# Causal convolution stage: twelve tap products per tile on ScalarE, three more unsplit input tiles, the mean of six chunks on VectorE

## The chip, the cores and the metric

One NeuronCore of a Trainium2 chip runs the whole program. The metric is the device time of one execution in microseconds (us), as the median of several runs. Engines are named as in the profile: PE (TensorE, matmul; PEld is its weight load), DVE (VectorE), ACT (ScalarE), POOL (GpSimd) and SP (SyncE). ACT, DVE, PE, POOL and SP each carry out their own instructions in the order in which the program was laid out.

## The reference

256 tokens of 2048 features pass through two blocks. The first block is a conformer convolution with a gated feed-forward layer, on 272 rows (16 meta tokens are put in front); the second has attention, pooling and a product-key expert layer. The change lies in the convolution:

```python
def conformer_conv(h, w_in, b_in, w_dw, b_dw, ln_g, ln_b, w_out, b_out):
    u = h @ w_in + b_in
    a, g = jnp.split(u, 2, axis=-1)
    u = a * jax.nn.sigmoid(g)
    u = jnp.pad(u, ((0, 0), (CONV_WIDTH - 1, 0), (0, 0)))
    u = lax.conv_general_dilated(u, w_dw[:, None, :], ...) + b_dw
    u = layer_norm(u, ln_g, ln_b)
    u = jax.nn.silu(u)
    return u @ w_out + b_out
```

CONV_WIDTH is 31 and the convolution is depthwise: every channel has 31 taps of its own.

## The kernel before, in words

**Tiles.** Channels lie on partitions, tokens along the free dimension. The convolution stage (`conv_stage`, L338) runs 16 iterations, one per group i of 128 channels. Iteration i makes two matmul products of 128x272: tile 2i (the half a) and tile 2i+1 (the gate g). Each contracts 2048 features in 16 steps, and its weights come as two units of 128x1024 (512 KB): tile m uses the units 2m and 2m+1. The iterations' products are called a(i) and g(i) here.

**Split and unsplit.** A split tile has its weights written as high part plus low part: ACT rounds the unit (L69), DVE subtracts (L84), and PE makes three products per step (L410 to L412). An unsplit tile goes to PE as it came (L414), with no work on ACT or DVE. `W_IN_SPLIT` (L41) names the split tiles: 4, 6, ..., 30, so a(2) to a(15) are split, and a(0), a(1) and all g(i) are not.

**Weights in flight.** `Weights` (L46) keeps four buffers for units as loaded (NRAW) and seven for split ones. SP issues the loads in order (L61); a load waits until its buffer is free, which for a split unit is after L84 and for an unsplit one after PE's last product with it. `split_to` (L71) splits ahead of need.

**Evacuation.** `evac` (L420) takes the sigmoid on ACT (L425, sg) and multiplies on DVE (L427), which writes the padded tile `up`. It is called sg(i) and up(i) here.

**Taps.** In iterations 2 to 14, 8 of the 31 taps are products on ACT (L445, `products`): four into a buffer of `wk["a"]`, four into one of `wk["b"]`, and a DMA issued by POOL adds the second to the first (L447). The other 23 taps run on DVE (L465, L467, then L470 alternating between two accumulators, joined at L472). `finish(i)` (L449) folds the four partial sums on DVE with three additions (L452, L453, L454); in the loop it is called for the tile before. Iterations 0 and 1 have all 31 taps on DVE. The last, i = 15, has 16 taps as products with diagonal matrices on PE (`diagonal_taps`, L480, L485) and 15 on DVE; there `finish(14)`, `taps(15)` and `finish(15)` (L456 its last addition) are called in this order behind up(15) (L533 to L541).

**Moments and normalisation.** Sums and sums of squares of each tile go into two accumulators, by a DMA up to i = 11 and by PE for the others (L501, L503). After the last one the mean and the root are formed (L561 on, an order written out by hand). For chunks k from KM = 4 on, POOL issues six DMAs that add the negative mean to two chunks each (L568 to L570), and `scale` (L553) only multiplies; for chunks below KM DVE multiplies and adds. Silu and a split of the result follow (L559, L192, L193), and the next matmul, `w_out`, begins.

**Order.** Instructions are ordered per engine when the program is built: by priority, with splits and evacuations moved ahead (`high_priority`), among those that the builder expects to be ready. That order is fixed on the chip.

Of the kernel before, what the change touches and what calls it, by code (L numbers as in the profile page):

```python
# [6 lines left out]
F32 = mybir.dt.float32  # L7
# [3 lines left out]
ALU = mybir.AluOpType  # L11

P = 128
# [12 lines left out]


NUP, LAG = 4, 3
NACT = [0, 0] + [8] * 13 + [0]
NPE = {15: 16}  # L30
NA, NB2 = 3, 2
MDMA = 11
KM = 4
SPE, SPL, SPM, HI, SPL2 = 65, 66, 67, 70, (68, 68, 68, 69, 70, 70, 70, 70)

HG, HM, HS, HC2, HT, HV = 19, 38, 14, 6, 24, 8
# [1 line left out]
CH, BU = 4, 2.7  # L38
U1 = 120
ENDS = (0, 0, 512), (1, 0, 256), (1, 256, 256)  # L40
W_IN_SPLIT = range(4, 32, 2)  # L41
COLS = ["mix_pre", "b_a", "b_g", "b_dw", "ln_g", "ln_b", "b_out", "mix_post",
        "ffn_pre", "ffn_post", "n1", "n2", "misc"]

# [51 lines left out]
class Kern:  # L96
# [238 lines left out]
    def w_in_split(self, i):  # L335
        return i in W_IN_SPLIT

    def conv_stage(self):  # L338
        nc, A, W = self.nc, self.A, self.W
        with ExitStack() as ctx:  # L340
            pl = ctx.enter_context(self.tc.tile_pool(name="p1", bufs=1))
# [15 lines left out]
            sq = pl.tile([P, TM], F32, name="sq1")  # L357
            r1 = pl.tile([P, TM], F32, name="r1")
            acc2 = pl.tile([P, 2, TM], F32, name="acc2")
            for k in range(0, KD, 2):  # L360
                g = self.col("mix_pre")
                nc.scalar.activation(hg[:, k], h[:, k], AF.Copy, scale=g[:, k:k + 1])
                nc.vector.tensor_scalar(hg[:, k + 1], h[:, k + 1], g[:, k + 1:k + 2], None, op0=ALU.mult)
                if k == 0:
                    nc.scalar.activation(acc2, h[:, :2], AF.Square)
                else:
                    s2 = self.tmp.tile([P, 2, TM], F32, tag="sq", name=self.nm("sq"), bufs=2)
                    nc.scalar.activation(s2, h[:, k:k + 2], AF.Square)
                    nc.vector.tensor_tensor(out=acc2, in0=acc2, in1=s2, op=ALU.add)
# [16 lines left out]
            for b in range(NUP):  # L386
# [10 lines left out]
                                           in1=self.col("b_dw"), op0=ALU.mult, op1=ALU.add)  # L397
# [3 lines left out]
            def product(i):  # L401
                ps = self.acc()
                t = t0 + 2 * i
                for k in range(KD):
                    u, o = t + k // UB, (k % UB) * P
                    W.split_to(u)
                    if self.w_in_split(i):
                        wh, wl = W.H(u, o), W.L(u, o)
                        uh, ul = uhl[:, k, :TM], uhl[:, k, TM:]
                        nc.tensor.matmul(ps[:, :TM], wh, uh, start=k == 0, stop=False)  # L410
                        nc.tensor.matmul(ps[:, :TM], wh, ul, start=False, stop=False)
                        nc.tensor.matmul(ps[:, :TM], wl, uh, start=False, stop=k == KD - 1)  # L412
                    else:
                        nc.tensor.matmul(ps[:, :TM], W.raw[u][:, o:o + P], (hg if i < 4 else h)[:, k], start=k == 0,  # L414
                                         stop=k == KD - 1)
                        if k % UB == UB - 1:
                            W.load_to(u + NRAW)
                return ps

            def evac(i, pa, pg):  # L420
                sg = self.tmp.tile([P, 2 * TM], F32, tag="sq", name=self.nm("sg"), bufs=2)[:, :TM]
                if i < 2:
                    for ps in (pa, pg):
                        nc.vector.tensor_tensor(out=ps[:, :TM], in0=ps[:, :TM], in1=r1, op=ALU.mult)
                x = nc.scalar.activation(sg, pg[:, :TM], AF.Sigmoid, bias=self.col("b_g")[:, i:i + 1])  # L425
                up = ups[i % NUP]
                y = nc.vector.scalar_tensor_tensor(out=up[:, 30:], in0=pa[:, :TM], scalar=self.col("b_a")[:, i:i + 1],  # L427
                                                   in1=sg, op0=ALU.add, op1=ALU.mult)
                return x, y

            def tap(i, j):
                return ups[i % NUP][:, 16 + j:16 + j + T], dw[:, i, j:j + 1]

            def products(i):

                wk[i] = wk["a"][i % len(wk["a"])]
                for j0 in range(31 - NACT[i], 31, 4):
                    if j0 == 31 - NACT[i]:
                        pr = wk[i]
                    else:  # L440
                        pr = wk["b"][wk["n"] % len(wk["b"])]
                        wk["n"] += 1
                    for j in range(j0, j0 + 4):
                        x, w = tap(i, j)
                        nc.scalar.activation(pr[:, j - j0], x, AF.Copy, scale=w)  # L445
                    if j0 > 31 - NACT[i]:
                        nc.gpsimd.dma_start(out=wk[i], in_=pr, accum_op=ALU.add)  # L447

            def finish(i):  # L449
                if NACT[i]:  # L450
                    a, c = wk[i], conv[:, i]
                    nc.vector.tensor_tensor(out=a[:, :2], in0=a[:, :2], in1=a[:, 2:], op=ALU.add)  # L452
                    nc.vector.tensor_tensor(out=a[:, 0], in0=a[:, 0], in1=a[:, 1], op=ALU.add)  # L453
                    nc.vector.tensor_tensor(out=c, in0=c, in1=a[:, 0], op=ALU.add)  # L454
                if i in NPE:
                    return nc.vector.tensor_tensor(out=conv[:, i], in0=conv[:, i], in1=wk["p", i][:, :T],  # L456
                                                   op=ALU.add)

            def taps(i, j0=0, j1=31):

                c, s, n = conv[:, i], (conv[:, i], acc2[:, 0, :T]), 31 - NACT[i] - NPE.get(i, 0)
                for j in range(j0, min(n, j1)):
# [11 lines left out]
            def diagonals(i, j0, j1):  # L474
                for j in range(j0, j1):
                    d = wk["d"].pop()
                    nc.scalar.activation(d, self.ident, AF.Copy, scale=dw[:, i, j:j + 1])
                    wk[i, j] = d

            def diagonal_taps(i):  # L480

                js = range(31 - NACT[i] - NPE[i], 31 - NACT[i])
                wk["p", i] = self.acc()
# [9 lines left out]
            wk = {"n": 0}  # L493
# [12 lines left out]
            for i in range(16):  # L506
                pa = product(2 * i)
                if i < 15:
                    W.split_to(t0 + 4 * i + 5)
                pg = product(2 * i + 1)  # L510
                W.split_to(t0 + min(4 * i + 7, SPE))
                with self.tc.high_priority(offset=PRIO + (300 if i == 15 else 0)):
                    x, y = evac(i, pa, pg)
                if i == 15:
                    break
                if i == 1:
                    t = self.xp.tile([P, 8192], F32, tag="X", name="work")
                    chunk = lambda r: t[:, 1024 * r:1024 * r + 1024].rearrange("p (q t) -> p q t", q=4)
                    wk["a"], wk["b"] = [chunk(r) for r in range(NA)], [chunk(r) for r in range(NA, NA + NB2)]
                    wk["d"] = [t[:, o:o + P] for o in range(1024 * (NA + NB2), 7936, P)]  # L520
                    wk["m"] = [t[:, 7936:], acc2[:, 1, :T]]
                    for w, v in enumerate((0.0, D * 1e-5 / P)):
                        nc.vector.memset(wk["m"][w], v)
                if i == 14:
                    diagonals(15, 31 - NPE[15], 31)
                if NACT[i]:
                    products(i)
                taps(i)
                if i > 0:
                    finish(i - 1)  # L530
                if i >= LAG:
                    moments(i - LAG)
# [20 lines left out]
            def scale(k, w):  # L553
                c = conv[:, k:k + w]
                for op, t in ((ALU.mult, rb), (ALU.add, mb))[:1 if k >= KM else 2]:
                    nc.vector.tensor_tensor(out=c, in0=c, in1=t.unsqueeze(1).to_broadcast([P, w, T]), op=op)
# [4 lines left out]
            with self.tc.high_priority(offset=3 * PRIO), self.tc.manual_schedule(engines=ORDERED), \  # L561
# [3 lines left out]
                a, c = acc2[:, 0, :T], [conv[:, k] for k in range(4)]  # L565
                nc.vector.scalar_tensor_tensor(out=v, in0=mom[1], scalar=1.0 / D, in1=v, op0=ALU.mult, op1=ALU.subtract)
                nc.scalar.activation(mn, mom[0], AF.Copy, scale=-1.0 / D)
                for k in range(KM, KD, 2):  # L568
                    nc.gpsimd.dma_start(out=conv[:, k:k + 2], in_=mn.unsqueeze(1).to_broadcast([P, 2, T]),
# [936 lines left out]
```

## Time and profile before

| what | value |
|---|---|
| median of 3 runs | 3250.02 us (3248.82 to 3256.38) |
| profiled execution, its own time | 3248.8 us |
| its span on the core | 3246.9 us |
| mean granted TensorE clock | 0.995 of full speed |
| PE busy | 3213.8 us, 99% |
| DVE busy | 2313.5 us, 71% |
| ACT busy | 1740.9 us, 54% |
| POOL busy | 39.8 us, 1% |

The span is the time from the first to the last profiled instruction; the profiled execution's own time is 1.9 us longer. Busy times overlap between engines, and the idle time of one engine costs something only when it moves the end. Times below count from the start of the span.

### The profile page before, as it was taken

Reading aid. Unit: us, or ns where it says so; the run is one execution under the profiler, and the core shown is the slowest. Engines: PE = TensorE matmul, PEld = TensorE weight load, DVE = VectorE, ACT = ScalarE, POOL = GpSimd, SP = SyncE. Lnnn points to the kernel's source line nnn. Section 1 sums busy time; section 2 is a strip of 40 time slices with the busy share of each in tenths; the row PEclk is TensorE's granted clock in tenths of the full one; section 3 lists DMA queues with packets and bytes.
Section 4 is the critical chain, followed back from the end, with each engine's and each line's share of the span. In section 5 each row is a group of like instructions: output and inputs, shape, how many; then the busy total and the mean of one; then the engine's idle time right before and its main releaser. Section 6 shows DMA issues by size and latency. Waiting matters only on the chain.

```text
span 3246.9 us, 49725 instructions
## 1 busy us (share of the span) xinstructions
PE 3213.8 (99%) x18613; PEld 2826.3 (87%) x18613; DVE 2313.5 (71%) x4106; ACT 1740.9 (54%) x2951; POOL 39.8 (1%) x47
## 2 busy tenths in 40 slices
PE   9989999999999999999999999999999999999999
PEld 8978888888888889999988888888888888888888
DVE  8997765666666766665569997777776676666664
ACT  4446644444444644544355467777877444444442
POOL 0110000000000000000000000000000000000000
PEclk9999999999999999999999999999999999999999
DMA  6787465555655555555655667777777977777764
GB/s 205 203 204 219 161 189 188 187 187 190 188 186 186 175 182 176 176 175 182 202 188 178 202 213 227 226 229 234 231 227 239 316 261 247 241 246 232 232 197 155
DMA packets 244002, 672.14 MB, mean 207 GB/s; under 512 B 21920, under 2 KB 95152, under 8 KB 241456
## 3 DMA queue, kind: packets, MB, share of 16 engines
q1 hardware_dynamic: 211968, 616.09, 59.8%
q10 hardware_dynamic: 24832, 41.34, 3.4%
q0 software_dynamic: 6960, 11.54, 2.0%
q8 instruction: 146, 2.39, 0.3%
q14 instruction: 96, 0.79, 0.1%
HBM read 619.58 MB, written 37.77 MB: 202 GB/s over the span
## 4 chain that ended last, share of the span: by engine, by line
PE 92%; DVE 5%; DMA 2%; ACT 1%; issue 0%; SPq 0%; ACTq 0%; DVEq 0%
PE acc L168 33%; PE acc L169 17%; PE acc L1392 7%; PE acc L1391 7%; PE acc L1390 7%; PE acc L175 4%; PE acc L177 4%; PE acc L176 4%; PE acc L414 3%; DVE wh L84 1%; PE g L1327 1%; DVE conv L470 1%; DMA wr<-in_w_in_dram 1%; DVE acc L470 1%; PE acc L937 0%; PE acc L938 0%
## 5 line engine op out<-in xcount | busy, mean ns | idle before, releaser
L84 DVE TENSOR_TENSOR wh<-wr,wh 128x1024 fp32r<-128x1024 f32 x1062 | 1295.8, 1223 | 735.8 <-ACT wh L69 733.2
L69 ACT ACTIVATE wh<-wr 128x1024 fp32r<-128x1024 f32 x1062 | 1123.4, 1060 | 1269.0 <-PE acc L169 426.7
L168 PE MATMUL acc<-xn,wh 128*128 128x512 f32 x2301 | 807.9, 394 | 0.0
L169 PE MATMUL acc<-xn,wh 128*128 128x256 f32 x2301 | 643.5, 280 | 0.0
L168 PEld LDWEIGHTS acc<-xn,wh 128*128 128x128 f32 x2301 | 431.3, 187 | 94.2
L168 PE MATMUL acc<-n,wh 128*128 128x512 f32 x1405 | 494.6, 397 | 0.0
L169 PEld LDWEIGHTS acc<-xn,wh 128*128 128x128 f32 x2301 | 434.4, 189 | 0.0
L1391 PE MATMUL acc<-wh,hid 128*128 128x512 f32 (+1 forms) x1032 | 399.8, 387 | 0.0
L1392 PE MATMUL acc<-wh,hid 128*128 128x512 f32 (+1 forms) x1032 | 399.8, 387 | 0.0
L1390 PE MATMUL acc<-wh,hid 128*128 128x512 f32 (+1 forms) x1032 | 399.7, 387 | 0.0
L169 PE MATMUL acc<-n,wh 128*128 128x256 f32 x1405 | 394.5, 281 | 0.0
L168 PEld LDWEIGHTS acc<-n,wh 128*128 128x128 f32 x1405 | 264.9, 189 | 63.1
L169 PEld LDWEIGHTS acc<-n,wh 128*128 128x128 f32 x1405 | 266.5, 190 | 0.1
L175 PE MATMUL acc<-n,wh 128*128 128x256 f32 x899 | 258.6, 288 | 7.0 <-ACT n L657 7.0
L176 PE MATMUL acc<-n,wh 128*128 128x256 f32 x899 | 255.7, 285 | 0.0
L177 PE MATMUL acc<-n,wh 128*128 128x256 f32 x899 | 253.3, 285 | 0.0
L168 PE MATMUL acc<-mid,wh 128*128 128x512 f32 x693 | 244.4, 398 | 0.0
L1390 PEld LDWEIGHTS acc<-wh,hid 128*128 128x128 f32 x1032 | 193.8, 188 | 39.7
L1391 PEld LDWEIGHTS acc<-wh,hid 128*128 128x128 f32 x1032 | 193.8, 188 | 39.6
L1392 PEld LDWEIGHTS acc<-wh,hid 128*128 128x128 f32 x1032 | 193.8, 188 | 39.6
L169 PE MATMUL acc<-mid,wh 128*128 128x256 f32 x693 | 193.9, 280 | 0.0
L175 PEld LDWEIGHTS acc<-n,wh 128*128 128x128 f32 x899 | 174.0, 194 | 13.1 <-ACT n L657 7.8
(379 smaller groups left out, 4410.0 us busy)
## 6 DMA issues: line engine op xcount, KB each, us to landing
wr<-in_U_dram SPq DMA_DIRECT2D x256, 512.0 KB, 4.4
wr<-in_V_dram SPq DMA_DIRECT2D x256, 512.0 KB, 4.4
wr<-in_gate_dram SPq DMA_DIRECT2D x88, 512.0 KB, 3.6
wr<-in_up_dram SPq DMA_DIRECT2D x88, 512.0 KB, 3.6
wr<-in_down_dram SPq DMA_DIRECT2D x88, 512.0 KB, 3.6
wr<-in_w_out_dram SPq DMA_DIRECT2D x64, 512.0 KB, 4.6
wr<-in_gl_dram SPq DMA_DIRECT2D x64, 512.0 KB, 3.7
wr<-in_w_in_dram SPq DMA_DIRECT2D x63, 512.0 KB, 4.8
```

The lines of the kernel that those rows point to most:

```text
L69: self.K.nc.scalar.activation(self.hl[i][:, 0], self.raw[i], AF.Copy)
L84: nc.vector.tensor_tensor(out=h[:, 1], in0=r, in1=h[:, 0].bitcast(F32), op=ALU.subtract)
L168: nc.tensor.matmul(ps[:m, :2 * n], self.W.H(t, o, m), x[:, :2 * n], start=first, stop=False)
L169: self.mm = nc.tensor.matmul(ps[:m, :n], self.W.L(t, o, m), x[:, :n], start=False, stop=last)
L175: nc.tensor.matmul(ps[:, :n], self.W.H(t, o), x[:, :n], start=first, stop=False)
L176: nc.tensor.matmul(ps[:, :n], self.W.L(t, o), x[:, :n], start=False, stop=False)
L177: self.mm = self.end = nc.tensor.matmul(ps[:, :n] if one else ps[:, n:2 * n], self.W.H(t, o), x[:, n:2 * n], start=False, stop=last)
L414: nc.tensor.matmul(ps[:, :TM], W.raw[u][:, o:o + P], (hg if i < 4 else h)[:, k], start=k == 0, stop=k == KD - 1)
L470: nc.vector.scalar_tensor_tensor(out=t, in0=x, scalar=w, in1=t, op0=ALU.mult, op1=ALU.add)
L1390: nc.tensor.matmul(ps[:, :w], xh, wh, start=ee == 0, stop=False)
L1391: nc.tensor.matmul(ps[:, :w], xh, wl, start=False, stop=False)
L1392: nc.tensor.matmul(ps[:, :w], xl, wh, start=False, stop=ee == G - 1)
```

## The change

The three parts are these. Taps: iterations 2 to 14 have 12 taps as products on ACT; the third group of four stays in its own buffer, and `finish` adds it to the first on DVE in one 128x1024 addition. `wk["b"]` has three buffers for it, used in turn, and two of the diagonal matrices move to a new tile `dg`. Split: tiles 8, 16 and 24, which are a(4), a(8) and a(12), are no longer split. Mean: KM is 6, so chunks 4 and 5 get the mean on DVE and POOL issues five DMAs.

```diff
-NACT = [0, 0] + [8] * 13 + [0]
+NACT = [0, 0] + [12] * 13 + [0]
 NPE = {15: 16}
-NA, NB2 = 3, 2
+NA, NB2 = 3, 3
 MDMA = 11
-KM = 4
+KM = 6
...
-W_IN_SPLIT = range(4, 32, 2)
+W_IN_SPLIT = [i for i in range(4, 32, 2) if i % 8]
...
+            dg = pl.tile([P, 2, P], F32, name="dg")
...
                 wk[i] = wk["a"][i % len(wk["a"])]
-                for j0 in range(31 - NACT[i], 31, 4):
-                    if j0 == 31 - NACT[i]:
+                for n, j0 in enumerate((27, 23, 19)):
+                    if n == 0:
                         pr = wk[i]
                     else:
                         pr = wk["b"][wk["n"] % len(wk["b"])]
...
                     for j in range(j0, j0 + 4):
                         x, w = tap(i, j)
                         nc.scalar.activation(pr[:, j - j0], x, AF.Copy, scale=w)
-                    if j0 > 31 - NACT[i]:
+                    if n == 1:
                         nc.gpsimd.dma_start(out=wk[i], in_=pr, accum_op=ALU.add)
+                    elif n == 2:
+                        wk["c", i] = pr

             def finish(i):
                 if NACT[i]:
                     a, c = wk[i], conv[:, i]
+                    nc.vector.tensor_tensor(out=a, in0=a, in1=wk["c", i], op=ALU.add)
                     nc.vector.tensor_tensor(out=a[:, :2], in0=a[:, :2], in1=a[:, 2:], op=ALU.add)
...
-                    wk["d"] = [t[:, o:o + P] for o in range(1024 * (NA + NB2), 7936, P)]
+                    wk["d"] = [t[:, o:o + P] for o in range(1024 * (NA + NB2), 7936, P)] + [dg[:, j] for j in range(2)]
```

## Rows read from the trace of the kernel before

**Rows 1.** The page: span, and busy time of each engine.

```profile
span 3246.9 us, 49725 instructions
PE 3213.8 (99%) x18613; PEld 2826.3 (87%) x18613; DVE 2313.5 (71%) x4106; ACT 1740.9 (54%) x2951; POOL 39.8 (1%) x47
```

**Rows 2.** Busy time by stretch: PE, PEld, DVE, ACT, POOL; granted clock, DMA share, GB/s.

```profile
54.25:227.50 173.25, 173.25 (x1041) 156.59 (x1039) 169.49 (x387) 75.78 (x149) 31.48 (x36) 1.00 0.81 204
227.50:257.80 30.30, 18.05 (x94) 15.59 (x93) 29.84 (x71) 15.23 (x26) 4.62 (x7) 0.83 0.57 146
```

**Rows 3.** The chain that ended last: a(0) to g(1), g(2), g(3), g(4) (start, us, what).

```profile
21.12 19.82 PE acc L414 x86
...
46.92 7.33 PE acc L414 x32
60.25 7.33 PE acc L414 x32
73.58 7.33 PE acc L414 x32
```

**Rows 4.** PE in order of time: the last product g(15), diagonals, moments, w_out.

```profile
220.01 7.50 PE L414 MATMUL acc<-h,wr 128*128 128x272 f32 x32
239.03 9.14 PE L485 MATMUL acc<-up,work 128*128 128x256 f32 x32 [11.52 <-DVE up L427]
248.01 0.59 PE L491 MATMUL mom<-work,ones 128*128 128x256 f32 x2
252.35 0.70 PE L503 MATMUL mom<-conv,ones 128*128 128x256 f32 x2 [0.73 <-DVE conv L456]
257.78 0.36 PE L175 MATMUL acc<-silu,wh 128*128 128x256 f32 x1
```

**Rows 5.** ACT in order of time: sg(3), sg(4) and sg(14) with what stands before them.

```profile
70.94 1.06 ACT L69 ACTIVATE wh<-wr 128x1024 fp32r<-128x1024 f32 x1 [7.83 <-DMA wr<-in_w_in_dram]
71.91 0.47 ACT L425 ACTIVATE sg<-acc,cols 128x272 f32<-128x272 f32 x1
...
84.53 0.47 ACT L425 ACTIVATE sg<-acc,cols 128x272 f32<-128x272 f32 x1
...
223.70 1.06 ACT L69 ACTIVATE wh<-wr 128x1024 fp32r<-128x1024 f32 x1 [4.96 <-DMA wr<-in_w_out_dram]
224.66 0.47 ACT L425 ACTIVATE sg<-acc,cols 128x272 f32<-128x272 f32 x1
...
228.77 2.09 ACT L445 ACTIVATE work<-up,dw 128x256 f32<-128x256 f32 x5
```

**Rows 6.** DVE in order of time: a tap, a folding addition, a split, the next.

```profile
214.69 0.48 DVE L470 SCALAR_TENSOR_TENSOR conv<-up,dw,conv 128x256 f32<-128x256 f32 x1
215.08 0.68 DVE L452 TENSOR_TENSOR work<-work 128x512 f32<-128x512 f32 x1
215.68 1.22 DVE L84 TENSOR_TENSOR wh<-wr,wh 128x1024 fp32r<-128x1024 f32 x1
216.82 0.42 DVE L472 TENSOR_TENSOR conv<-conv,acc 128x256 f32<-128x256 f32 x1
```

**Rows 7.** DVE in order of time: up(14), up(15), finish(14), end of finish(15), scale(4).

```profile
225.93 0.50 DVE L427 SCALAR_TENSOR_TENSOR up<-acc,cols,sg 128x272 f32<-128x272 f32 x1
...
238.49 0.48 DVE L427 SCALAR_TENSOR_TENSOR up<-acc,cols,sg 128x272 f32<-128x272 f32 x1
...
243.22 0.67 DVE L452 TENSOR_TENSOR work<-work 128x512 f32<-128x512 f32 x1
...
251.88 0.42 DVE L456 TENSOR_TENSOR conv<-conv,acc 128x256 f32<-128x256 f32 x1
...
259.90 0.42 DVE L193 TENSOR_TENSOR silu<-conv,silu 128x256 fp32r<-128x256 f32 x1
260.46 0.69 DVE L556 TENSOR_TENSOR conv<-conv,r 128x512 f32<-128x512 f32 x1
```

**Rows 8.** POOL's DMA of tile 14, and landing times of these DMAs (median, 100 to 275 us).

```profile
231.16 0.86 POOL L447 DMA_DIRECT2D work<-work  x1 [10.89 <-ACT work L445]
work<-work POOLq DMA_DIRECT2D x10, 512.0 KB, 10.2
```

**Rows 9.** The chain that ended last, after the moments: the mean's DMA, scale, silu.

```profile
254.04 6.39 DMA conv<-r
260.46 0.70 DVE conv L556
...
263.10 0.50 PE acc L168
```

**Rows 10.** Granted clock in stretches (columns as in rows 2): the diagonals run here.

```profile
240.00:241.00 1.00, 1.00 (x4) 0.78 (x3) 1.00 (x3) 1.00 (x2) 0.00 (x0) 0.50 0.10 16
243.00:244.00 1.00, 1.00 (x6) 0.86 (x5) 1.00 (x3) 0.42 (x1) 0.00 (x0) 0.98 0.28 29
```

**Rows 11.** Weight loads, 180 to 215 us, and the longest in the chain that ended last.

```profile
DMA to landing us min/median/max: 3.9/5.2/9.9
...
176.06 10.70 DMA wr<-in_w_in_dram
```

## The prediction

> **What bounds the kernel now.** I read the page first. PE is busy 3213.8 of 3246.9 us [rows 1], so everything that is to be won is 33.1 us of PE idle time, plus whatever PE does slowly. The busy times by stretch say where it lies. From 54 to 227.5 us PE never stops; beside it DVE is busy 169.5 of 173.25 us and ACT only 75.8. From 227.5 to 257.8 PE works 18.05 of 30.3 us, at a mean clock of 0.83, while DVE is busy 29.84 [rows 2]. So there are two stages with two limits: PE while the input products run, DVE in the tail after them. What shortens DVE's list during the products wins nothing there; it counts only if the tail gets shorter.
>
> PE in order of time shows the tail: g(15) ends at 227.5, and the diagonal products wait 11.5 us for up(15) [rows 4]. Why up(15) is so late stands in ACT's order. The period is 73.58 - 60.25 = 13.33 us [rows 3], so g(14) ended at 214.2, but sg(14) ran at 224.66, 10.5 us late: in front of it stands the rounding of a weight unit needed two tiles on, which waited for its DMA [rows 5]. At the beginning, behind the unsplit a(0) and a(1), the delay was smaller: g(3) ended at 67.6 and sg(3) ran at 71.9, g(4) at 80.9 and sg(4) at 84.5 [rows 3, 5], 4.3 and 3.6 us. The delay is built up by splitting, and a late sg(14) makes up(14), its ACT products, their DMA and finish(14) late. That is the chain I follow.
>
> **Unsplit tiles.** An unsplit tile takes 7.33 us of PE, a split one 13.33 - 7.33 = 6.00 [rows 3]. Three tiles: 3 x 1.33 = 4.0 us more, and nothing hides it, for PE has no idle time there [rows 2]. The products end at 231.5 instead of 227.5.
>
> The Trainium skill (FP8 and Floating Point Precision, TensorE Precision Notes) says that a true fp32 product takes four passes through the array. Against the three products of a split step that would make 6.00 x 4/3 = 8.0 us a tile, 6.0 us in all, and a time 2.0 us later than mine; the trace does not agree, with 7.33, and the measured number decides.
>
> In return six splits go: on DVE 6 x 1.14 = 6.8 us (from the start of a split to that of the next instruction) [rows 6], on ACT 6 x 1.06 = 6.4 [rows 5]. Their worth is indirect: sg(2), sg(6) and sg(10) no longer have a rounding in front of them, and the delay starts anew from there.
>
> The number of loads that SP issues is unchanged, but the buffers of a(4), a(8) and a(12) now come free only as PE uses them, so the next split tile's units arrive later behind them on SP. The first can load 3.67 us into the tile (half of 7.33); it needs its landing, 1.06 for the rounding and 1.14 for the subtraction by 14.66 (two unsplit tiles). Landings take 3.9 to 9.9 us, 5.2 in the median, at worst 10.7 [rows 11]; 8.8 are allowed. Cost: 0 by the median, 1.9 us by the worst; the second unit, free at 7.33 and needed at 14.66 + 3.00, 2.6 by the worst. I take 0, since these two loads go out 3.67 us apart and not in a bunch.
>
> **Taps.** Per tile DVE loses four taps at 0.39 us and gets one 128x1024 addition. No such addition is in the trace; the nearest row is the split, a two-operand instruction of that size, 1.14. Twice the 128x512 addition would be 1.20 [rows 6]. I take 1.14: 1.56 - 1.14 = 0.42 us saved, 5.5 over 13 tiles. With the splits DVE is relieved of 12.3 us, enough to catch up with a PE that became 4 us slower. ACT gets 52 products at 2.09 / 5 = 0.42 us [rows 5], 21.7 us, into 97.5 us of idle time [rows 2]. DMAs are as many as before, and POOL's issue still follows the eighth product. A new wait: the second group of four writes a buffer that DVE's finish two tiles before must have read. If DVE is behind, ACT stands there, with the next roundings queued behind it: 0 to some 3 us a tile, inside ACT's idle time. I take 0.
>
> **The mean.** DVE gets one addition of 128x512, 0.60 us [rows 6], in front of silu(4). What it saves is the wait for the first DMA, which landed at 260.43 [rows 9]: DVE's instruction before ran from 259.90 to 260.32, scale(4) began at 260.46 [rows 7]. So 0.14 goes and 0.60 comes, and PE was waiting for just that chunk at 263.10 [rows 9]. Later DMAs move up by one place, which gives some of it back. Bounds: 0.3 gained to 0.6 lost; I take 0.3 lost.
>
> **The sum.** g(14) ends at 231.5 - 13.33 = 218.2. Tile 24 is the last unsplit one, two iterations before 14, as a(1) is before 3; so I take the delay of sg(3) and sg(4), 4.0 us, and not 10.5: sg(14) at 222.2. up(14) follows 1.27 later, as before [rows 5, 7], at 223.5. POOL issued tile 14's DMA 231.16 - 225.93 = 5.2 us after up(14), and these DMAs land in 10.2 [rows 7, 8]: 238.9. finish(14) comes before taps(15) in the program, so DVE waits there; before, it began at 243.22. From there to the last addition of finish(15) it was 251.88 - 243.22 = 8.66 us [rows 7]; with the new addition 9.8. That gives 248.7 instead of 251.88, 3.2 us earlier. PE must keep up: behind up(15) 9.14 us of diagonals and 3.6 of moments [rows 4] ask for up(15) by about 235.5; 12.56 us after up(14), as before [rows 7], is 236.1, less 0.42 saved. It just fits. With the mean: 3.2 - 0.3 = 2.9 us won. Behind this stage PE is the limit, so the gain stays to the end: 3248.8 - 2.9 = 3245.9 for the profiled execution. The median of the runs lies 1.2 above that execution: **3247 us**.
>
> A measurement of this kernel can tell about 0.3% from no change, 9.75 us. The forecast lies within it.
>
> **Rivals.**
>
> *A: the evacuation becomes prompt.* If no rounding stands in front of sg(14), up(14) comes 1 us behind its product, at 219.2, and the DMA lands at 234.6: 244.4, 7.5 us earlier. If taps(15) run while finish(14) waits, up(15) at 232.5 is the start, and the diagonals follow an idle time of 1.5 us instead of 11.5. Before, they ran at half clock, 1.2 GHz, until 243 and at full clock after it [rows 10]. At the spacing of the moments' products, 3.6 us for eight [rows 4], 16 diagonals take 7.2: the last moments can begin at 232.5 + 0.5 + 7.2 + 3.6 = 243.8 instead of 252.35, 8.5 earlier, the best that this rival gives. Time: **3242**. For it: DVE is relieved of 12.3 us. Against it: sg(3), soon after unsplit tiles, was already behind a rounding [rows 5].
>
> *B: the delay stays (slower).* One place: the rounding in front of sg(14), whose DMA lands late. At 10.5 us of delay up(14) comes at 230.0, the DMA lands at 245.4 and the end is at 255.2, 3.3 later: 3250 + 3.3 + 0.3 = **3253.6**. It turns into a loss from a delay of 7.2 us on. For it: 10.5 us were standing at sg(14), and ACT's order is fixed when the program is built. Against it: the delay needs splits one after another to grow, and only a(13) to a(15) follow tile 24.
>
> *C: PE starves behind the unsplit tiles.* With the worst landing, 10.7, PE waits 2.6 us after each of three tiles, 7.8: 3254.9 with the forecast's tail, **3261** with B's. It decides from a landing of 8.8 us on. Against it: the loads are spaced, and behind g(1), which ended at 40.9, g(2) began at 46.92 [rows 3], after the 6.0 us of a(2) and no wait.
>
> **How the numbers follow.** Forecast 0.50, A 0.25, B 0.15, C 0.10. The likeliest gives 3247. Its range reaches to A's best end, 8.5 us and the mean's 0.3 below 3250 with some 0.7 for the spread of the runs, on one side, and past B on the other; only C with B lies outside: 3240.5 to 3254. Over 0.3% faster needs A's best end and a favourable mean, 0.06; over 0.3% slower needs C with B, 0.06; the rest, 0.88, is within.
>
> **What would show it.** Right: PE's products end near 231.5, with no idle time before; DVE shows 13 additions of 128x1024 near 1.2 us and is idle at times before 227; sg(14) some 4 us behind g(14); an idle time of DVE before finish(14)'s first addition, ended by a DMA; the last addition of finish(15) near 248.7; no DMA wait at scale(4). A shows in an idle time of PE before the diagonals of under 2 us and a clock that stays up. B shows in a DMA wait of ACT before sg(14) with 8 us or more. C shows in idle PE at the starts of a(5), a(9), a(13). The forecast is wrong if the tail from the products' end to the w_out product, 30.3 us before [rows 2, 4], is not between 21 and 28.

## The result: slower by 1.2%, and the profile after

The changed kernel is called after, and the runs of the experiments are numbered 1 to 13.

| | before | after |
|---|---|---|
| median of the runs beside each other (4 each) | 3250.64 us | 3288.59 us |
| ratio, 95% interval | | 1.0121 [1.0100, 1.0142] |
| span of the profiled execution | 3246.9 us | 3282.4 us |

The forecast was 3247 us, the range 3240.5 to 3254, and "slower" had a chance of 0.06. It is outside.

The page of the kernel after, span and busy time of each engine, answers to [rows 1]:

```profile
span 3282.4 us, 49624 instructions
...
PE 3225.3 (98%) x18565; PEld 2829.1 (86%) x18565; DVE 2304.7 (70%) x4062; ACT 1755.2 (53%) x2997; POOL 38.7 (1%) x46
```

DVE has 8.8 us less work and PE 11.5 us more, but the span grew by 35.5 us: most of it is idle time. Busy time by stretch (PE, PEld, DVE, ACT, POOL; then granted clock, DMA share, GB/s) shows where, against [rows 2]:

```profile
54.25:227.50 173.25, 155.04 (x829) 136.02 (x829) 143.69 (x313) 77.96 (x169) 30.02 (x35) 0.95 0.70 179
227.50:257.80 30.30, 25.67 (x149) 22.45 (x147) 17.78 (x36) 8.73 (x17) 0.86 (x1) 1.00 0.51 137
```

PE, which had no idle time in the first stretch, now has 18.2 us of it, and DVE, which was meant to be relieved, is idle for 29.6 us instead of 3.8. Who waits, and for what, stands in the list of waits of DVE and of PE, 40 to 330 us (total, times, longest):

```profile
DVE work L456 <- DMA work<-work: 38.6, 7, 7.5
...
PE acc L490 <- DVE up L428: 14.1, 1, 14.1
PE acc L411 <- ACT wh L69: 11.2, 1, 11.2
PE acc L413 <- DVE wh L84: 8.0, 5, 3.6
PE mom L508 <- DVE conv L461: 3.5, 1, 3.5
```

L456 is the new 128x1024 addition, now the first instruction of `finish`. In seven tiles DVE stands there for the DMA that adds the second group of products to the first. The same list of the kernel before names no wait for that DMA. One period of after shows it, DVE in order of time (start, duration, instruction, idle time before it and what ended it): up(9), its last tap, finish(9), up(10).

```profile
167.76 0.49 DVE L428 SCALAR_TENSOR_TENSOR up<-acc,cols,sg 128x272 f32<-128x272 f32 x1
...
176.36 0.49 DVE L475 SCALAR_TENSOR_TENSOR conv<-up,dw,conv 128x256 f32<-128x256 f32 x1
182.98 1.23 DVE L456 TENSOR_TENSOR work<-work 128x1024 f32<-128x1024 f32 x1 [6.13 <-DMA work<-work]
...
185.63 0.43 DVE L459 TENSOR_TENSOR conv<-conv,work 128x256 f32<-128x256 f32 x1
185.98 0.50 DVE L428 SCALAR_TENSOR_TENSOR up<-acc,cols,sg 128x272 f32<-128x272 f32 x1
```

POOL's issue of tile 9's DMA in after, and for comparison that of tile 11 (the tenth of 13) in the kernel before:

```profile
172.84 0.86 POOL L449 DMA_DIRECT2D work<-work  x1 [4.05 <-ACT work L447]
```

```profile
190.13 1.05 POOL L447 DMA_DIRECT2D work<-work  x1 [10.23 <-ACT work L445]
```

In after DVE is through with its taps 4.0 us behind the issue (176.85 against 172.84) and has nothing in front of finish(9). In the kernel before, finish(11) is the row at 215.08 in [rows 6], 25 us behind its DMA's issue, so a landing of 10 us never made DVE wait. The DMA did not become slower (8.6 us in the median of ten in after, 10.2 before [rows 8]); DVE came earlier. The order of DVE's instructions in the two traces says the same: before, finish(i) stands behind up(i+2) and amid the last taps of tile i+1, because DVE had a backlog of taps. In after, from tile 6 on, it stands directly behind the taps of tile i and ahead of up(i+1).

The period of that tile is 185.98 - 167.76 = 18.2 us, against 13.33 of PE [rows 3]. How long DVE stands follows the landing, the time from the issue of the DMA to its completion. Landing times of the adding DMAs issued at 172.84, 190.11 and 206.01 us (each the only one of its stretch; last number):

```profile
work<-work POOLq DMA_DIRECT2D x1, 512.0 KB, 10.0
```

```profile
work<-work POOLq DMA_DIRECT2D x1, 512.0 KB, 7.7
```

```profile
work<-work POOLq DMA_DIRECT2D x1, 512.0 KB, 4.5
```

The waits of DVE behind them are 6.13 us, 3.89 us and none, which is the landing less the 4 to 5 us of work that DVE still had behind the issue. What becomes of such a wait shows around 200 us, in DVE, then ACT, then PE of after:

```profile
197.95 1.23 DVE L456 TENSOR_TENSOR work<-work 128x1024 f32<-128x1024 f32 x1 [3.89 <-DMA work<-work]
...
200.60 0.42 DVE L459 TENSOR_TENSOR conv<-conv,work 128x256 f32<-128x256 f32 x1
```

```profile
201.06 0.42 ACT L503 ACTIVATE s<-conv 128x256 f32<-128x256 f32 x1 [9.65 <-DVE conv L459]
201.38 0.47 ACT L426 ACTIVATE sg<-acc,cols 128x272 f32<-128x272 f32 x1
202.42 4.90 ACT L447 ACTIVATE work<-up,dw 128x256 f32<-128x256 f32 x12 [0.57 <-DVE up L428]
207.23 1.99 ACT L69 ACTIVATE wh<-wr 128x1024 fp32r<-128x1024 f32 x2
```

```profile
195.63 1.54 PE L415 MATMUL acc<-h,wr 128*128 128x272 f32 x6
208.32 0.60 PE L411 MATMUL acc<-uhl,wh 128*128 128x272 f32 x1 [11.15 <-ACT wh L69]
```

finish ends at 201.0; ACT's square (L503) waits for it, sg(11) stands behind the square, then come the twelve products and then the roundings for a(13). PE, through with g(12), stands for 11.15 us. Each engine is in order, so one late instruction on DVE holds up ACT's and PE's next work.

The sum goes by the end of the last moments and of the products, and by the first w_out product. PE of the kernel before, the row behind the one at 252.35 in [rows 4], then PE of after:

```profile
252.89 0.67 PE L503 MATMUL mom<-s,ones 128*128 128x256 f32 x2
```

```profile
246.64 7.50 PE L415 MATMUL acc<-h,wr 128*128 128x272 f32 x32
...
286.16 0.98 PE L508 MATMUL mom<-s,ones 128*128 128x256 f32 x2
...
292.69 0.36 PE L175 MATMUL acc<-silu,wh 128*128 128x256 f32 x1
```

The last moments end at 253.6 us before and at 287.1 in after: the products end at 254.1 instead of 227.5, 26.6 later, of which 4.0 are the longer unsplit tiles, 19.2 are waits of PE (11.2 and 8.0 in the list) and 3.4 are left. Part of the rest is the clock: after the wait of 11.15 us the granted clock was 0.50 from 208 to 211 us and 0.54 from 211 to 215, the 1.2 GHz level, and 1.00 again from 215 to 219. The tail from the products' end to the last moments grew from 26.1 to 33.0. There ACT of after shows a rounding ahead of sg(14), as in [rows 5], and DVE a wait at finish(14):

```profile
250.12 1.06 ACT L69 ACTIVATE wh<-wr 128x1024 fp32r<-128x1024 f32 x1 [4.33 <-DMA wr<-in_w_out_dram]
251.08 0.47 ACT L426 ACTIVATE sg<-acc,cols 128x272 f32<-128x272 f32 x1
```

```profile
274.21 1.23 DVE L456 TENSOR_TENSOR work<-work 128x1024 f32<-128x1024 f32 x1 [6.01 <-DMA work<-work]
```

### The profile page after: what moved, and what is told of

Read it like the earlier page. It is cut to its first block, busy times and chain, and to the rows that moved or that the text cites. A ratio compares the mean times of both kernels' runs of the same rounds, so it can differ in the third digit from the quotient of the medians.

```text
span 3282.4 us, 49624 instructions
## 1 busy us (share of the span) xinstructions
PE 3225.3 (98%) x18565; PEld 2829.1 (86%) x18565; DVE 2304.7 (70%) x4062; ACT 1755.2 (53%) x2997; POOL 38.7 (1%) x46
## 4 chain that ended last, share of the span: by engine, by line
PE 90%; DVE 4%; DMA 3%; issue 2%; ACT 1%; POOL 0%; SPq 0%; POOLq 0%; DVEq 0%; ACTq 0%
PE acc L168 33%; PE acc L169 17%; PE acc L1397 7%; PE acc L1395 7%; PE acc L1396 7%; PE acc L175 4%; PE acc L177 4%; PE acc L176 4%; PE acc L415 2%; DMA work<-work 1%; PE g L1332 1%; DVE wh L84 1%; PE acc L942 0%; PE acc L944 0%; PE acc L943 0%
```

## The experiments

In the expectations, theory 1 is the order on DVE and the wait for the adding DMA, theory 2 the units behind unsplit tiles that arrive too late for PE, theory 3 the twelve products on ACT that hold up the roundings, unless a run names others.

**One part alone (1 to 3).** The kernel before with one part of the change each.

```diff
-W_IN_SPLIT = range(4, 32, 2)
+W_IN_SPLIT = [i for i in range(4, 32, 2) if i % 8]
```

> The kernel before with only tiles 8, 16 and 24 unsplit. Theory 1 (DVE stands at the first addition of finish, because DVE caught up with PE and the adding DMA, some 10 us long, has not landed): here DVE is relieved of 6.8 us and PE is 4 us longer, so waits of DVE for that DMA begin late in the stage, 5 to 20 us in all; time 3252 to 3268. Theory 2 (unsplit tiles free their buffers late, the next split tile's units come late and PE starves): nearly the whole loss is here, 3278 to 3290, with PE idle behind a(4), a(8) and a(12) and no DVE wait for the adding DMA. Theory 3 (twelve products on ACT hold up the roundings behind them): only PE's longer products, about 3254.

For the second, the whole taps part (12 products, three buffers, the new addition) with the splits and KM as before.

> The kernel before with only the tap change (12 products, third group added by DVE). Theory 1: DVE is relieved of 5.5 us spread over 13 tiles, so its backlog mostly stays and the waits for the adding DMA are few, under 10 us in all; time 3248 to 3260. Theory 2: no unsplit tiles, so about 3248 to 3251. Theory 3: nearly the whole loss is here, 3275 to 3290, with PE waiting for splits whose rounding stood behind products on ACT.

```diff
-KM = 4
+KM = 6
```

> The kernel before with KM = 6 only. All theories: 3250 to 3252, the w_out product 0.1 to 0.5 us later behind the moments than before, no DMA wait at the scaling of chunks 4 and 5.

Splits alone: 3269.04 us, 1.0061 [1.0044, 1.0078]. Taps alone: 3264.84, 1.0044 [1.0027, 1.0060]. Mean alone: 3250.02 against 3248.08, 1.0003 [0.9993, 1.0012]. The differences are 21.0, 16.8 and 1.9 us, together 39.7, where the whole change cost 38.0: two parts that have nothing in common but that they relieve DVE lose about the same. Both lost more than theory 1 expected, the first by 1 us only: 3269 where it had at most 3268, and 3265 where it had at most 3260, with more waiting (25.1 and 22.1 us) than the 5 to 20 and the under 10 expected. In the list of waits of DVE, first of the splits alone, then of the taps alone, the same line appears; in the first, with no new addition at all:

```profile
DVE work L452 <- DMA work<-work: 25.1, 5, 6.2
```

```profile
DVE work L456 <- DMA work<-work: 22.1, 5, 5.8
```

In both, finish(i) moves ahead of up(i+1), from tile 7 on in the first and from about tile 10 on in the second. Theories 2 and 3 can't explain both, since the second has no more unsplit tiles than before and the first no more products on ACT.

**Calling finish later (4).** After, with `finish(i - 2)` called ahead of `products(i)` instead of `finish(i - 1)` behind `taps(i)`.

```diff
+                if i > 1:
+                    finish(i - 2)
                 if NACT[i]:
                     products(i)
                 taps(i)
-                if i > 0:
-                    finish(i - 1)
...
+                finish(13)
                 finish(14)
```

> The changed kernel with finish of a tile called two iterations later, ahead of the products, instead of one iteration later behind the taps: the same work, the same DMAs, but the adding DMA has some 13 us more before DVE needs it. Theory 1: DVE's waits for the adding DMA fall from 38.6 us to under 5, PE's waits during the input products from some 19 us to under 5, time 3244 to 3258. Theory 2: the buffers are as before, time 3280 to 3290. Theory 3: the products on ACT are as before, time 3280 to 3290.

3279.3 us, 1.0091 [1.0074, 1.0108]. The edit did not do what it was for: finish(i) still stood ahead of up(i+1) in tiles 6 to 12, and DVE still waited 27.8 us for the DMA. Where a call stands in the program doesn't fix the order, so this run decides nothing.

**An order edge (5).** After, with finish(i-1) bound behind the last tap of tile i by an order edge, which fixes the order of two instructions and adds no work (`taps` returns its last addition).

```diff
-                taps(i)
+                e = taps(i)
                 if i > 0:
-                    finish(i - 1)
+                    with self.tc.issue_after(e.ins):
+                        finish(i - 1)
```

> The changed kernel with one thing more: finish of tile i-1 may not be issued on DVE before the last tap of tile i (an order edge, no other work). In the run with the late call the builder had still put finish of tile i ahead of up(i+1) from tile 6 on, so that run did not test the order. Theory 1 (in that place DVE, and behind it the next evacuation, stand until the adding DMA of some 10 us has landed): the waits of DVE for the adding DMA are left at finish(14) alone, under 8 us instead of 38.6, PE waits under 3 us during the input products, time 3241 to 3253. Theory 2 (late buffers behind the unsplit tiles): PE still waits behind a(4), a(8) and a(12), time over 3265.

3254.95 against 3248.61 us, 1.0021 [1.0009, 1.0033]: with nothing changed but the order, a loss of 38.0 us became one of 6.3. Theory 1 had expected a little more, at most 3253 us and under 3 us of PE's waits, which were 3.9. The list of waits of DVE has one such wait left, at finish(14):

```profile
DVE work L456 <- DMA work<-work: 2.3, 1, 2.3
```

**The order of after in the kernel before (6).** `finish(i)` right behind `taps(i)`, and the next evacuation bound behind it.

```diff
...
-                if i > 0:
-                    finish(i - 1)
+                finish(i)
...
-                finish(14)
```

> The kernel before, same work, with finish of tile i forced ahead of up(i+1) on DVE, as the builder placed it in the changed kernel. Theory 1: each tile then makes a loop of up, eight products on ACT, the adding DMA of 10 us, finish and the next up, some 18 us instead of 13.3; less the 11 us that the evacuation was late anyway, 30 to 50 us are lost: 3278 to 3300, with 12 or 13 DVE waits for the adding DMA. Theory 2: nothing is unsplit here, so 3248 to 3256.

3258.51 us, 1.0032 [1.0022, 1.0042]: slower, but by 10 us, not by 30 to 50. The list of waits of DVE in this run:

```profile
DVE work L452 <- DMA work<-work: 2.8, 4, 0.9
```

The landings of these DMAs from 100 to 275 us (count, size, median), against the 10.2 of [rows 8]:

```profile
work<-work POOLq DMA_DIRECT2D x11, 512.0 KB, 5.6
```

The expectation missed because it took the landing of 10 us as given. Here finish(i) has 21 of the longer taps (L470) in front of it instead of 17, and the DMA lands in 5.6. So this order does not make the loss by itself: it needs a landing longer than the work that DVE has in front of finish, and the landing was another here. What the order would cost the kernel before at a landing of 10 us was not measured. The 10 us that were lost lie mostly in the tail: the products ended at 230.0, 2.5 us later than before, but up(15), bound behind finish(14), came at 250.2 instead of 238.5. What goes with the landing is in the last section.

**No DMA to wait for (7).** After, with all three groups in buffers of their own and both additions on DVE; eight more of the diagonal matrices move to `dg`.

```diff
-                        nc.gpsimd.dma_start(out=wk[i], in_=pr, accum_op=ALU.add)
+                        wk["e", i] = pr
...
+                    nc.vector.tensor_tensor(out=a, in0=a, in1=wk["e", i], op=ALU.add)
```

> The changed kernel with the second group of products added by DVE too, in one more 128x1024 addition per tile, and no adding DMA for the taps. DVE gets 13 x 1.14 = 15 us more. Theory 1: no DVE wait for a DMA of tap products, no PE waits over 1 us each, time 3243 to 3260 although DVE has more to do. Theory 2: over 3270.

3249.83 against 3248.61 us, 1.0005 [0.9996, 1.0015]. DVE got 13 more additions, and the loss of 38.0 us became one of 1.2, though the unsplit tiles, the twelve products on ACT and the mean are all still there. So these did not make the loss; in this form they cost no more than that. It is no faster than before either, for DVE is as full as it was (columns as above):

```profile
54.25:227.50 173.25, 171.78 (x962) 151.88 (x961) 170.86 (x358) 86.73 (x187) 20.89 (x24) 1.00 0.58 167
```

Whether the missing DMA or the fuller DVE took the loss away, this run can't tell, since in the kernel before a DVE that full met no wait. Run 5 tells it: there DVE's work is that of after and only the order differs.

**The edge with one part each (8, 9).** The order edge of run 5 on the splits alone and on the taps alone.

> The kernel before with tiles 8, 16 and 24 unsplit, as in the run that changed only this (3269), and the same order edge on finish. Theory 1: 3242 to 3254. Theory 2: 3265 to 3272, as without the edge.

> The kernel before with twelve products (third group added by DVE) and the order edge that keeps finish of tile i-1 behind the last tap of tile i; all splits as before. Without the edge this took 3265. Theory 1, now with the landing time in it (finish waits for the adding DMA, which takes 4.7 us with no weight load issued just before it and 10 us behind four of them): no DVE wait for that DMA but at finish(14), PE without waits during the input products, up(15) 3 to 6 us earlier than in the kernel before; time 3243 to 3251. If the twelve products on ACT cost something by themselves (theory 3), PE waits for splits remain and the time is over 3255.

Splits: 3253.54 us, 1.0014 [1.0005, 1.0024], instead of 3269 without the edge. Taps: 3243.98 against 3246.58, 0.9992 [0.9983, 1.0000], instead of 3264.8. In both most of the loss goes with the edge, and what is left of it belongs to the splits. In run 9 PE has no wait for a split at all, with the twelve products on ACT, so theory 3 falls here.

**The tail (10, 11).** Runs 9 and 5, with taps(15) ahead of finish(14), so that its DMA has time to land.

```diff
-                finish(14)
-                taps(15)
-                z = finish(15)
+                e = taps(15)
+                with self.tc.issue_after(e.ins):
+                    finish(14)
+                    z = finish(15)
```

> The same, and taps(15) ahead of finish(14), so that the last wait for the adding DMA is covered too. Theory 1: no DVE wait for the adding DMA at all, 1 to 3 us less than the run beside it, 3241 to 3250. If the time is bound elsewhere in the tail (diagonals on PE behind up(15)), the same time as the run beside it.

> The changed kernel with the order edge, and taps(15) ahead of finish(14). With the edge alone it took 3255, DVE stood 2.3 us at finish(14). Theory 1: 1 to 3 us less, 3251 to 3255; what is left above the kernel before is the longer unsplit tiles (4.0 us) and PE's waits behind a(8) and a(12) (6 us). If those waits came from the adding DMA after all, they shrink too.

3243.75 us, 0.9992 [0.9983, 1.0001], and 3255.24, 1.0027 [1.0018, 1.0036]: neither differs from its parent by more than the intervals, so the 1 to 3 us that theory 1 expected were not won. DVE's waits of 2.6 and 2.3 us at finish(14) are gone from both traces, and the time is not: in both DVE then waits 2.2 us for PE's moments instead.

**What is left of after (12, 13).** In run 5 PE still waited for splits, 3.9 us in all, in a(9) and a(13). There up(i) stood behind all taps of tile i-1 and a finish. Now up(i) is bound behind the first 8 taps of tile i-1 only, the other taps behind up(i), finish(i-2) behind them; run 12 on after, run 13 on the taps alone. The edit against after, with J1 = 8:

```diff
+                if i > 2:
+                    with self.tc.issue_after(y.ins):
+                        e = taps(i - 1, J1)
+                    with self.tc.issue_after(e.ins):
+                        finish(i - 2)
                 if NACT[i]:
                     products(i)
-                taps(i)
-                if i > 0:
-                    finish(i - 1)
+                e = taps(i, 0, J1 if i > 1 else 31)
...
-                finish(14)
-                taps(15)
+                e = taps(14, J1)
+                with self.tc.issue_after(e.ins):
+                    finish(13)
+                    finish(14)
+                    taps(15)
```

> The changed kernel with an order on VectorE in which up(i) stands behind only the first 8 taps of tile i-1, then the other taps of i-1, then finish(i-2). Theory 1 (what is left after the order edge is again the order: up(i) stands behind all taps of tile i-1 and a finish, so the sigmoid's tile comes late, and with it the roundings and splits behind it): up(7) and up(8) come within 4 us of the end of g(7) and g(8), the 2.21 us wait of TensorE for a split in a(9) goes, the products end at 231 to 233 (4.0 us of longer unsplit tiles remain), time 3246 to 3252. Theory 2 (the two units behind an unsplit tile land too late, whatever VectorE does): the waits at the starts of a(9) and a(13) stay, products end at 235 to 238, time 3253 to 3257. Theory 3 (twelve products on ScalarE hold the roundings): the waits stay too, but named as waits for L69, with the roundings right behind 12 products.

> The same order on VectorE in the version with the twelve products alone (tiles 8, 16, 24 split, mean as before). Theory 1: products end at 226 to 228 with no wait of TensorE, up(15) within 5 us of that; the tail then holds 11 more taps of tile 14, 4.3 us, so the last moments end at 248 to 252; time within 4 us of the kernel before, on either side. If up(15) is no earlier than in the version with the order edge alone (233.8), theory 1 is wrong about what holds it, and the time is 3248 to 3252.

Run 12: 3256.03 against 3248.32 us, 1.0021 [1.0011, 1.0032], no better than run 5 and above the 3246 to 3252 expected, though the part of the expectation about PE came true. Busy time by stretch, columns as above, then PE and ACT in order of time, in the tail:

```profile
54.25:227.50 173.25, 173.25 (x976) 153.81 (x975) 151.59 (x334) 89.26 (x188) 31.84 (x36) 1.00 0.76 201
```

```profile
228.61 2.68 PE L415 MATMUL acc<-h,wr 128*128 128x272 f32 x11
239.88 2.08 PE L490 MATMUL acc<-up,dg 128*128 128x256 f32 x4 [8.58 <-DVE up L428]
...
258.37 1.22 PE L508 MATMUL mom<-conv,ones 128*128 128x256 f32 x2 [4.85 <-DVE conv L461]
```

```profile
222.80 1.71 ACT L447 ACTIVATE work<-up,dw 128x256 f32<-128x256 f32 x4 [3.03 <-DVE work L456]
...
225.45 1.04 ACT L69 ACTIVATE wh<-wr 128x1024 fp32r<-128x1024 f32 x1
226.39 0.47 ACT L426 ACTIVATE sg<-acc,cols 128x272 f32<-128x272 f32 x1
```

PE is busy for the whole stretch, and its products end at 231.3, where the forecast had them, 231.5. So with this order neither the units behind the unsplit tiles nor the products on ACT held PE up. In run 5 the products did hold up roundings. ACT of run 5, then of run 11, the products of up(7) and the roundings for a(9):

```profile
130.14 4.89 ACT L447 ACTIVATE work<-up,dw 128x256 f32<-128x256 f32 x12 [0.57 <-DVE up L428]
134.94 1.99 ACT L69 ACTIVATE wh<-wr 128x1024 fp32r<-128x1024 f32 x2
```

```profile
126.54 4.90 ACT L447 ACTIVATE work<-up,dw 128x256 f32<-128x256 f32 x12 [0.57 <-DVE up L428]
131.34 1.04 ACT L69 ACTIVATE wh<-wr 128x1024 fp32r<-128x1024 f32 x1
132.92 1.06 ACT L69 ACTIVATE wh<-wr 128x1024 fp32r<-128x1024 f32 x1 [0.54 <-DMA wr<-in_w_in_dram]
```

In run 5 both roundings stand behind the products and neither waits for a load, so the units were there; what was late is up(7), and PE waited 2.2 us in a(9). Run 11 has the same order as run 5 on DVE, ACT and PE up to the end of the products, but there up(7) came 3.6 us earlier and PE didn't wait in a(9); its waits were 0.8 us in all, and the products ended at 232.0, not 237.2. So these waits also vary from one execution to the next by some 3 us, and that run 12's order, with up(7) at 122.8, removes them for good is likely, not shown by one trace. Waits in a(9) or a(13) show in runs 7 (1.5 us) and 8 (3.7) too, and none in runs 9, 10 and 13, which keep all splits. So theories 2 and 3 are not the loss, but unsplit tiles, with products in front of the roundings behind them, were worth some 1 to 4 us.

In run 12 the last moments end at 260.4 all the same, 6.8 us behind before: 3.8 from the products and 3.0 from a tail of 29.1 us. In the tail sg(14) ran at 226.4, 8.4 us behind g(14) (218.0); in front of it stand four products that waited 3.03 us for a buffer that finish two tiles back had yet to read, and a rounding. DVE had 11 taps of tile 14 still to do behind up(15), 4.3 us that the expectation for this run left out, though that for run 13 had them. How much of the tail each of the three costs was not told apart.

Run 13: 3243.07 against 3248.32 us, 0.9987 [0.9978, 0.9996]; up(15) at 230.0 and the last moments at 251.1, as expected. It is the best version found: about 4 us, or 0.13%, by the ratio, less than the 0.3% that the prediction names as what a measurement can tell from no change. Its profiled execution, at 3251.68 us, was the longest of its eleven, so these two moments are not those of a median one.

## Why the prediction was wrong

**What failed.** The step that failed is in "Taps" and "The sum": DVE relieved of 12.3 us (the page shows 8.8 us less busy time, the mean's addition in it) was booked as a gain ("enough to catch up"), and the wait of finish for its DMA in tiles 2 to 13 was put at nothing. DVE did catch up, and so it met a wait that its backlog had covered, 38.6 us in seven tiles, finish(14) among them. The prediction knew the DMA (issue 5.2 us behind up, landing 10.2 [rows 7, 8]) and knew that DVE would wait for it at finish(14). For the other twelve tiles it kept the old place of finish without saying so. With its own numbers the loss could have been found: behind up(i) DVE has some 9 us of work (17 taps at 0.39, two shorter ones and a split; 167.76 to 176.85 in after), the DMA lands 5.2 + 10.2 = 15.4 us behind up(i), so 6 us of waiting; then some 3 us of finish, and a period of 18, five more than PE's 13.33. That is the tile shown; where the landing was shorter, DVE waited less. The prediction's own sign of being wrong showed: from the products' end to the first w_out product it was 38.6 us (254.1 to 292.7), not 21 to 28. And one of its signs of being right, DVE idle at times before 227 us, came as the loss itself, 29.6 us. The question that was not asked: if DVE is no longer behind, what stands next in its list, and is that ready?

**Unsplit tiles, right.** 4.0 us more on PE. Without PE's waits the products ended at 231.3 (run 12), against 231.5 forecast. The Trainium skill (FP8 and Floating Point Precision, TensorE Precision Notes) has four passes for a true fp32 product. The prediction's estimate from that rule, 8.0 us a tile, would have ended the products at 233.5; run 12 speaks for the measured 7.33. That is no evidence against four passes as such: the estimate also takes each of the three products of a split step to cost as much as one pass, which no run tests.

**Late units, taken as 0: too low by 1 to 4 us.** PE waited in a(9) and a(13), rival C's place, in runs 5, 7, 8 and 11, the runs with unsplit tiles in which the large wait is gone, for 3.9, 1.5, 3.7 and 0.8 us; only in run 12 it did not. C's mechanism, a load that lands too late, doesn't show in a(9) of run 5: there the units had landed, and the roundings stood behind the products of a late up(7).

**The delay of sg(14), wrong.** Forecast 4.0 us. It was 11.7 in after (g(14) ended at 239.4, sg(14) ran at 251.08) and 7.8 in run 11, where g(14) ended at 218.7. ACT in order of time, run 11, then run 9, where g(14) ended at 212.9:

```profile
225.58 1.06 ACT L69 ACTIVATE wh<-wr 128x1024 fp32r<-128x1024 f32 x1 [4.45 <-DMA wr<-in_w_out_dram]
226.54 0.47 ACT L426 ACTIVATE sg<-acc,cols 128x272 f32<-128x272 f32 x1
```

```profile
219.10 1.06 ACT L69 ACTIVATE wh<-wr 128x1024 fp32r<-128x1024 f32 x1 [4.52 <-DMA wr<-in_w_out_dram]
220.06 0.47 ACT L426 ACTIVATE sg<-acc,cols 128x272 f32<-128x272 f32 x1
```

The reason given for 4.0 was that the delay grows by splitting and starts anew behind an unsplit tile. With the order edge it was 7.2 us in run 9, which keeps all splits, and 7.6 in run 5, which doesn't: the unsplit a(12) made it no shorter. The rounding in front of sg(14) is of a unit of w_out, in [rows 5] too, which PE needs only behind the moments, at 257.78 before [rows 4]; it waits for its load whatever is split. In run 13 that rounding waited for no DMA, and the delay was 3.7.

This is rival B's place, a rounding that waits for its DMA in front of sg(14). B had 0.15; it gave 3253.6, 3.6 above the kernel before, from a delay of 10.5, and became a loss from 7.2 on. Runs 5 and 11, in which the large loss is gone, came to 3255, 6.3 and 8.7 us above the kernel before beside them. So without the wait in DVE's list the time would have been nearer to B than to the forecast; how much of it is sg(14) and how much are PE's waits was not told apart.

**The new addition, right.** Taken as 1.14 us from the split; it runs 1.23, with 1.14 to the next instruction. The wait for a second group's buffer, taken as 0, was no matter in after, whose list of ACT's waits doesn't name it; it came up in run 12, 3.03 us in the row above.

**finish(14), right in kind.** DVE waits there for the DMA, 6.01 us in after, 2.3 in run 5. That removing it gains nothing (runs 10, 11) was not forecast.

**The mean, not contradicted.** Forecast 0.3 us lost; alone it measured 1.9, with an interval that holds zero and 0.3 alike. The wait for the first DMA of the mean is gone there, and no gain shows.

**The frame, half right.** "What shortens DVE's list during the products wins nothing there" held. That it can lose there was missing. The rivals for a slower outcome, B and C, looked at ACT, SP and PE, none at DVE, the engine that the change relieves.

## What to carry to other kernels

A backlog on an in-order engine hides the latency of whatever it will consume next. Before you lighten such an engine, list what it consumes from DMAs and from other engines, and work out how long after the issue it will get there without the backlog. Where the builder orders by expected readiness, bind the consumer of a slow transfer behind independent work with an order edge, and read the order off the built program, since moving the call may change nothing (run 4).

## What the runs showed of the hardware

**Landing behind weight loads.** The same DMA, 512 KB added to a buffer on the chip, landed in 4.5 to 12.5 us. Around the issue of the one of 10.0 us in after, at 172.84, SP issued four weight loads of 512 KB, three in the 5 us before it and one 0.2 us behind its start:

```profile
167.88 5.52 SPq L61 DMA_DIRECT2D wr<-in_w_in_dram  x4
```

Ahead of the one of 4.5 us there was none in that time. In the kernel before, too, four stood ahead of the one at 190.13, and it landed in 10.0; so that is the usual case there. Counted over the 182 such DMAs of 14 profiled runs, loads from 6 us before the start of POOL's issue to 1 us behind it: with none the median was 4.7 us (11 DMAs); with one 5.5 (27); with two 7.0 (16); with three 7.7 (71, from 4.6 to 11.9); with four 10.0 (57, none under 7.7). In run 6, where most had one load ahead and the next ones behind, they took 5.6. This is a count, not an experiment with loads alone, so that the loads are the cause is likely but not shown.

**A wait costs PE more than its length.** After 11.15 us of idle time PE of after began a(13) at 208.32, stood once more for 1.95 us, and worked at a granted clock of 0.50 to 0.54, the 1.2 GHz level, until 215 us, its products 0.23 us apart; only then came 1.00, the 2.4 GHz level, with 0.125 us between them.
